# Six half-size loads, one per weight tile, in place of three whole ones before the last projection

## The chip, the cores and the metric

The kernel runs on one core of one Trainium2 chip. Its time is the device time of one execution in microseconds (us), given as the median of several runs. The engines that matter here are TensorE (PE, matmuls), ScalarE (ACT), VectorE (DVE), GpSimd (POOL) and SyncE (SP). SP and ACT each have a queue through which transfers (DMAs) are issued; the transfers of both are carried out by the same 16 DMA engines.

## The reference

One decoder layer over 256 tokens of width 2048 in float32: three gated branches, merged and projected back, and then a gated embedding, on which this case turns.

```python
def mixer_layer(x, p_i, ...):
    h = rmsnorm(x, norm_g)
    proj = h @ w_in
    ...                                    # attention A, attention B, recurrence C
    y_d = jnp.einsum('bsnc,ncd->bsnd', y, w_br)
    merged = jnp.einsum('bsnd,bsnd->bsd', gates, y_d)
    x = x + merged @ w_out
    x = x + jax.nn.sigmoid(rmsnorm(x, ple_norm_g) @ w_pg) * (p_i @ w_pp)
    return x

def reference(x, p, ...):
    ...
    return rmsnorm(x, final_norm_g)
```

`p_i @ w_pp` depends on no earlier step, and `final_norm_g` is needed only at the very end.

## The kernel before, in words

Every float32 matrix product is made as three matmuls (L185 to L187) of values split into a high part and a residual. The weights stream from DRAM in tiles of 128 x 1024 (512 KB). Each tile goes the same way: `fetch` issues its DMA on SP's queue into one of five raw buffers (`r_...`), `split` casts the high part on ACT (L136, `wh_...`) and takes the residual on DVE (L138, `wl_...`) into one of four pairs of buffers, and PE makes 12 matmuls from it. A tile's raw buffer is free again when its residual is done, its high and residual buffers when PE is done with it.

The stretch that matters is the end of the output projection `w_out` and the start of the gate's projection `w_pg`. The second half of `w_out` (named `out2` in the source, `out` in the trace) has plain tiles in two column chunks; they are called here 0_4 to 0_14 and 1_4 to 1_14, after chunk and first row block. `w_pg` follows in four column chunks of eight tiles. In the first pass the tiles 0 to 5 of its chunk 0 run, then 0 to 5 of chunk 1, and after them 6 and 7 of both. The names of both chunks read `pg_0`, `pg_1` and so on once the buffer numbers are left out, so in each list below the second `pg_0` is that of the second chunk.

When a column chunk n of the output projection is finished (n = 0 to 3), `residual` adds it into `xr` on DVE (L1081) and sums squares on ACT (L1084, `jy`). `turn_later` then turns it into the layout that `w_pg` needs: two transposes on DVE (L808, `flip_x`), four DMAs into DRAM (L812, `d_x`), one DMA back (L813, `turn_x`), and some tiles later four scalings on ACT (L1011), a cast (L1012, `x_hi`) and a residual on DVE (L1013, `x_lo`). The DMA back waits on SP's queue until the four others have landed, and whatever stands behind it on that queue waits too.

The projection of p was made at the start and parked in DRAM (`pp_d`). Two blocks of 128 x 2048 (`pps`, 1 MB each) are loaded back, and one block `fg` with the final norm's weights repeated in every partition (1 MB). The last stage, `output` and `gated`, reads both.

The order around the change is set in two ways. Within the program text an operation can be put off: `later(ticks, work)` keeps it until `tick()` has been called that often, and `tick()` is called once per weight tile, after its split. All of it is then placed on the engines' queues by a scheduler, which follows its own estimate of the times; each engine runs its list strictly in that order. DMAs draw on eight shared completion semaphores in turn, and a DMA may have to wait until the one before it on the same semaphore has landed.

Of the kernel before, what the change touches and what calls it, by code (L numbers as in the profile page):

```python
# [16 lines left out]
P = 128  # L17
D = 2048
SEQ = 256
NH = SEQ // P  # L20
BW = D // 2
# [31 lines left out]
def trunk(ctx: ExitStack, tc: tile.TileContext, x, early, table, onehot, maskv, w_in, sinks, conv, w_ri, vec, fin, w_br,  # L53
          w_out, w_pg, out):
    nc = tc.nc
# [9 lines left out]
    def block(name, dtype=F32):  # L65
        return blk.tile([P, SLOT], dtype, tag="blk", name=name)
# [74 lines left out]
    def later(ticks, work):  # L141
        timers.append([ticks, work])
# [349 lines left out]
    pp_d = dram.tile([2, P, NH, BW], F32, name="pp_d")  # L492
# [458 lines left out]
    def wide(t):  # L951
        return t[:, : NH * BW].rearrange("p (h c) -> p h c", h=NH)
# [142 lines left out]
    rms_finish(rs2, tot)  # L1095

    pps = [wide(block(f"pp{h}")) for h in range(2)]
    for h in range(2):
        nc.scalar.dma_start(pps[h], pp_d[h])

    fg = block("fg")
    nc.scalar.dma_start(fg[:, :D], bass.AP(tensor=fin.tensor, offset=fin.offset, ap=[[0, P], [1, D]]))
    HW = CW // 2
    sq3 = const.tile([P, NH, 4], F32, name="sq3")
    part = const.tile([P, NH], F32, name="part")
# [180 lines left out]
```

## Time and profile before

| | us |
|---|---|
| median of three runs | 995.31 (993.62 to 995.84) |
| profiled execution, its own time | 993.94 |
| its span in the profile | 992.1 |
| PE busy | 978.4 (99%) |
| DVE busy | 700.0 (71%) |
| ACT busy | 583.2 (59%) |
| DMA moved | 232.63 MB, 234 GB/s over the span |

Busy times are shares of the span. A busy PE is not PE at full pace: the granted clock, one digit for each fortieth of the span, stands beside it. Times inside the span are counted from its start.

### The profile page before, as it was taken

What the parts mean: (1) busy time and instruction counts of PE and PEld (TensorE: products, weight loads), DVE (VectorE), ACT (ScalarE), POOL (GpSimd) and SP (SyncE); (2) the same over time, 40 slices, a digit from 0 to 9 for tenths busy, and PEclk for the clock granted to TensorE, in tenths of its full rate; (3) what the DMA queues carried; (4) which work ended last, traced back from release to release, by engine and by line L of the source; (5) the groups of instructions that cost most, each with busy time, mean ns of one, the idle gap of its engine ahead of it and who ended that gap; (6) DMA issues with size and microseconds to landing.
All of it is one profiled execution on the core that took longest, in us unless ns stands there. A gap on an engine that the chain in (4) does not pass through costs nothing.

```text
span 992.1 us, 12462 instructions
## 1 busy us (share of the span) xinstructions
PE 978.4 (99%) x4432; PEld 814.2 (82%) x4432; DVE 700.0 (71%) x983; ACT 583.2 (59%) x818; POOL 3.4 (0%) x12
## 2 busy tenths in 40 slices
PE   9999999999999999999999999999999999989996
PEld 7888888888888888888888888888888888868886
DVE  6746875566877576576567888697589598946583
ACT  7644545557676566545466766765556465746562
POOL 0000000000000000000000000000000000000000
PEclk9999999999999999999999999999999999989999
DMA  9967877777788667637888786677748966798552
GB/s 343 323 189 227 289 225 231 220 225 233 237 251 258 222 191 242 212 128 234 252 256 273 237 250 221 214 225 234 251 153 272 343 210 214 233 347 261 186 181 85
DMA packets 83494, 232.63 MB, mean 234 GB/s; under 512 B 9400, under 2 KB 30952, under 8 KB 82920
## 3 DMA queue, kind: packets, MB, share of 16 engines
q1 hardware_dynamic: 76896, 219.32, 68.1%
q10 hardware_dynamic: 6536, 12.52, 3.6%
q8 instruction: 35, 0.57, 0.2%
q14 instruction: 27, 0.22, 0.1%
HBM read 211.06 MB, written 20.75 MB: 234 GB/s over the span
## 4 chain that ended last, share of the span: by engine, by line
PE 94%; DMA 2%; DVE 2%; ACT 1%; issue 0%; SPq 0%; DVEq 0%; ACTq 0%
PE ps_in L186 21%; PE ps_in L187 21%; PE ps_in L185 21%; PE ps_pg L185 3%; PE ps_pg L186 3%; PE ps_pg L187 3%; PE ps_out L186 2%; PE ps_out L187 1%; PE ps_out L185 1%; PE ps_bra L186 1%; PE ps_bra L187 1%; PE ps_brc L185 1%; PE ps_brc L187 1%; PE ps_bra L185 1%; PE ps_brc L186 1%; PE ps_brb L185 1%
## 5 line engine op out<-in xcount | busy, mean ns | idle before, releaser
L138 DVE TENSOR_TENSOR wl_in<-r_in,wh_in 128x1024 fp32r<-128x1024 f32 x224 | 273.2, 1221 | 152.3 <-ACT wh_in L136 146.9
L136 ACT CAST wh_in<-r_in 128x1024 fp32r<-128x1024 f32 x224 | 235.1, 1052 | 204.9 <-PE ps_in L187 170.5
L186 PE MATMUL ps_in<-wl_in,h 128*128 128x512 f32 x896 | 349.1, 390 | 0.4 <-DVE wl_in L138 0.4
L185 PE MATMUL ps_in<-wh_in,h 128*128 128x512 f32 x896 | 349.3, 390 | 0.0
L187 PE MATMUL ps_in<-wh_in,h 128*128 128x512 f32 x896 | 349.0, 389 | 0.0
L186 PEld LDWEIGHTS ps_in<-wl_in,h 128*128 128x128 f32 x896 | 168.2, 188 | 34.8 <-DVE wl_in L138 0.8
L187 PEld LDWEIGHTS ps_in<-wh_in,h 128*128 128x128 f32 x896 | 168.2, 188 | 34.8
L185 PEld LDWEIGHTS ps_in<-wh_in,h 128*128 128x128 f32 x896 | 168.3, 188 | 34.1
L138 DVE TENSOR_TENSOR wl_pg<-r_pg,wh_pg 128x1024 fp32r<-128x1024 f32 x28 | 34.3, 1223 | 24.2 <-ACT wh_pg L136 22.4
L136 ACT CAST wh_pg<-r_pg 128x1024 fp32r<-128x1024 f32 x28 | 29.5, 1053 | 29.1 <-PE ps_pg L187 20.4
L185 PE MATMUL ps_pg<-wh_pg,x_hi 128*128 128x512 f32 (+1 forms) x120 | 45.0, 375 | 0.0
L186 PE MATMUL ps_pg<-wl_pg,x_hi 128*128 128x512 f32 (+1 forms) x120 | 45.0, 375 | 0.0
L187 PE MATMUL ps_pg<-wh_pg,x_lo 128*128 128x512 f32 (+1 forms) x120 | 45.0, 375 | 0.0
L185 PE MATMUL ps_out<-wh_out,m_hi 128*128 128x512 f32 x96 | 38.7, 403 | 2.7 <-ACT wh_out L136 2.7
L136 ACT CAST wh_out<-r_out 128x1024 fp32r<-128x1024 f32 x24 | 25.1, 1052 | 27.3 <-PE ps_out L187 12.8
L138 DVE TENSOR_TENSOR wl_out<-r_out,wh_out 128x1024 fp32r<-128x1024 f32 x24 | 29.2, 1218 | 14.4 <-ACT wh_out L136 14.4
L186 PE MATMUL ps_out<-wl_out,m_hi 128*128 128x512 f32 x96 | 38.7, 403 | 0.5 <-DVE wl_out L138 0.5
L187 PE MATMUL ps_out<-wh_out,m_lo 128*128 128x512 f32 x96 | 38.3, 399 | 0.0
L138 DVE TENSOR_TENSOR wl_brc<-r_brc,wh_brc 128x1024 fp32r<-128x1024 f32 x16 | 19.6, 1222 | 20.2 <-ACT wh_brc L136 20.2
L136 ACT CAST wh_brc<-r_brc 128x1024 fp32r<-128x1024 f32 x16 | 16.9, 1055 | 25.1 <-PE ps_in L187 25.1
L136 ACT CAST wh_brb<-r_brb 128x1024 fp32r<-128x1024 f32 x16 | 16.9, 1054 | 23.4 <-PE ps_brb L187 9.4
L138 DVE TENSOR_TENSOR wl_brb<-r_brb,wh_brb 128x1024 fp32r<-128x1024 f32 x16 | 19.3, 1218 | 11.1 <-ACT wh_brb L136 11.1
(362 smaller groups left out, 1356.3 us busy)
## 6 DMA issues: line engine op xcount, KB each, us to landing
r_in<-w_in_dram SPq DMA_DIRECT2D x228, 512.0 KB, 4.5
r_pg<-w_pg_dram SPq DMA_DIRECT2D x32, 512.0 KB, 4.5
r_out<-w_out_dram SPq DMA_DIRECT2D x28, 512.0 KB, 4.8
r_brc<-w_br_dram SPq DMA_DIRECT2D x16, 512.0 KB, 3.6
r_bra<-w_br_dram SPq DMA_DIRECT2D x16, 512.0 KB, 4.3
r_brb<-w_br_dram SPq DMA_DIRECT2D x16, 512.0 KB, 4.4
d_b<-flip_b SPq DMA_DIRECT2D x32, 96.0 KB, 2.9
turn_b<-d_b SPq DMA_DIRECT2D x8, 384.0 KB, 4.9
```

Source lines behind the costliest of these rows:

```text
L136: casts.append(nc.scalar.copy(hi[:, c], r[:, c]).ins)
L138: los.append(nc.vector.tensor_tensor(lo[:, c], r[:, c], hi[:, c].bitcast(F32), op=ALU.subtract).ins)
L185: nc.tensor.matmul(ps, ah, bh, start=first, stop=False, **more)
L186: nc.tensor.matmul(ps, ah, bl, start=False, stop=False, **more)
L187: nc.tensor.matmul(ps, al, bh, start=False, stop=last, **more)
```

## The change

The two loads of the parked projection and the one of the final norm's weights are cut into six of 128 x 1024 (512 KB). They are no longer issued where they stand in the program but put off with `later`: the first comes at the second tick from there on, which is that of the second tile of `w_pg`, and one more at each tile after it.

```diff
     pps = [wide(block(f"pp{h}")) for h in range(2)]
-    for h in range(2):
-        nc.scalar.dma_start(pps[h], pp_d[h])
-
     fg = block("fg")
-    nc.scalar.dma_start(fg[:, :D], bass.AP(tensor=fin.tensor, offset=fin.offset, ap=[[0, P], [1, D]]))
+    rows = [(pps[h][:, i, :], pp_d[h][:, i, :]) for h in range(2) for i in range(NH)]
+    rows += [(fg[:, i * BW : (i + 1) * BW], bass.AP(tensor=fin.tensor, offset=fin.offset + i * BW, ap=[[0, P], [1, BW]]))
+             for i in range(2)]
+    for n, (to, src) in enumerate(rows):
+        later(2 + n, lambda to=to, src=src: nc.scalar.dma_start(to, src))
```

The amount of data and the reading side stay as they are. On ACT's queue, around the end of the first column chunk of the output projection, there stands before (casts of weight tiles, and the three DMAs):

```order
L1012 CAST x_hi<-turn_x_7100 128x1024
L136 CAST wh_out_0_14_7310<-r_out_0_14_7308 128x1024
L1099 DMA pp_7473<-pp_d 128x2048
L1099 DMA pp_7474<-pp_d 128x2048
L1102 DMA fg<-fin_dram 128x2048
L136 CAST wh_out_1_4_7342<-r_out_1_4_7340 128x1024
L136 CAST wh_out_1_6_7360<-r_out_1_6_7358 128x1024
```

After the change the three DMAs are gone from there, and the casts of tiles 0_14 and 1_4 follow each other. On the same queue, at the first tiles of `w_pg` before:

```order
L136 CAST wh_pg_1_7505<-r_pg_1_7503 128x1024
L136 CAST wh_pg_2_7529<-r_pg_2_7527 128x1024
L136 CAST wh_pg_3_7547<-r_pg_3_7545 128x1024
L1084 ACTIVATE jy_7455,sq_6831<-xr_6822 128x512 x2
L136 CAST wh_pg_4_7565<-r_pg_4_7563 128x1024
L1011 ACTIVATE turn_x_7330<-turn_x_7330,vecs 128x2x4x32 x4
L136 CAST wh_pg_5_7583<-r_pg_5_7581 128x1024
L1012 CAST x_hi<-turn_x_7330 128x1024
L136 CAST wh_pg_0_7601<-r_pg_0_7599 128x1024
```

`turn_x_7330` is the turned chunk n = 2. The same place after the change:

```order
L136 CAST wh_pg_1_7502<-r_pg_1_7500 128x1024
L1011 ACTIVATE turn_x_7330<-turn_x_7330,vecs 128x2x4x32 x4
L136 CAST wh_pg_2_7527<-r_pg_2_7525 128x1024
L1012 CAST x_hi<-turn_x_7330 128x1024
L1103 DMA pp_7473<-pp_d 128x1024 x2
L136 CAST wh_pg_3_7546<-r_pg_3_7544 128x1024
L1103 DMA pp_7474<-pp_d 128x1024
L1084 ACTIVATE jy_7455,sq_6831<-xr_6822 128x512 x2
L136 CAST wh_pg_4_7565<-r_pg_4_7563 128x1024
```

The scalings of chunk n = 2 moved from behind the cast of tile 4 to ahead of that of tile 2, and the first three of the six DMAs stand around the cast of tile 3. The last two, on the same queue, with the semaphores that each row waits for (`DMAHW` and a number are those of DMAs):

```order
L1103 DMA fg<-fin_dram 128x1024 [waits DMAHW1_49]
L136 CAST wh_pg_0_7603<-r_pg_0_7601 128x1024 [waits DMAHW0_49,PE_49,Activation_49]
L1103 DMA fg<-fin_dram 128x1024 [waits DMAHW6_49]
L136 CAST wh_pg_1_7622<-r_pg_1_7620 128x1024 [waits DMAHW2_49,DVE_49,PE_49]
L136 CAST wh_pg_2_7646<-r_pg_2_7644 128x1024 [waits DVE_49,PE_49]
```

The second half of `fg` waits for semaphore 6, which the DMA of `r_pg_2` of the second chunk raises; so ACT reaches the cast of `pg_1` of that chunk only when that later tile has landed. On SP's queue, at the fetches of these tiles, before:

```order
L812 DMA d_x_7334<-flip_x_7331 32x4x256 x4
L110 DMA r_pg_3_7545<-w_pg_dram 128x1024
L110 DMA r_pg_4_7563<-w_pg_dram 128x1024
L110 DMA r_pg_5_7581<-w_pg_dram 128x1024
L110 DMA r_pg_0_7599<-w_pg_dram 128x1024
L813 DMA turn_x_7330<-d_x_7334 128x1024
L110 DMA r_pg_1_7617<-w_pg_dram 128x1024
```

And after the change:

```order
L812 DMA d_x_7462<-flip_x_7459 32x4x256 [waits DMAHW0_49]
L812 DMA d_x_7462<-flip_x_7459 32x4x256 [waits DMAHW2_49]
L812 DMA d_x_7462<-flip_x_7459 32x4x256 [waits DMAHW3_49]
L110 DMA r_pg_3_7662<-w_pg_dram 128x1024 [waits DMAHW4_49,DVE_49]
L110 DMA r_pg_4_7680<-w_pg_dram 128x1024 [waits DMAHW5_49,DVE_49]
```

These are the last three transfers of chunk n = 3 and the two fetches behind them. Semaphore 2 is raised by `r_pg_1` of the second chunk, 3, 4 and 5 by the second, third and fourth of the new loads, so SP waits there for ACT's transfers to land. Further up on the same queue `turn_x_7330` now stands right behind the fetch of tile 3, with tiles 4, 5 and 0 behind it:

```order
L110 DMA r_pg_3_7544<-w_pg_dram 128x1024
L813 DMA turn_x_7330<-d_x_7334 128x1024
L110 DMA r_pg_4_7563<-w_pg_dram 128x1024
L110 DMA r_pg_5_7582<-w_pg_dram 128x1024
L110 DMA r_pg_0_7601<-w_pg_dram 128x1024
```

It moved ahead of those three fetches.

## The prediction

> **What bounds the kernel now.** I read the page first, for the engine that carries the end and for the slice where it does not.
>
> ```profile
> PEclk9999999999999999999999999999999999989999
> DMA  9967877777788667637888786677748966798552
> PE 94%; DMA 2%; DVE 2%; ACT 1%; issue 0%; SPq 0%; DVEq 0%; ACTq 0%
> ```
>
> TensorE (PE) is 94% of the chain that ended last, so a change pays only where PE stands still or runs slowly. The granted clock leaves 9 in one slice alone, the 36th of 40 (24.8 us each: 868 to 893 us), which is also a slice in which the DMA engines are at 9. The waits between 850 and 993 us name what PE lacks there.
>
> ```profile
> ACT wh_out L136 <- DMA r_out<-w_out_dram: 10.6, 2, 10.1
> PEld ps_out L185 <- ACT wh_out L136: 3.2, 1, 3.2
> PE ps_out L185 <- ACT wh_out L136: 2.7, 1, 2.7
> ```
>
> ScalarE (ACT) waited 10.1 us at one stroke for a weight tile of w_out, and PE waited 2.7 us for that cast. PE's own timeline gives the whole price; these are the last matmul before the gap, the first two behind it, the first back at full pace, and a later one.
>
> ```profile
> 875.69 0.39 PE L187 MATMUL ps_out<-wh_out,m_lo 128*128 128x512 f32 x1
> 878.82 0.76 PE L185 MATMUL ps_out<-wh_out,m_hi 128*128 128x512 f32 x1 [2.74 <-ACT wh_out L136]
> 880.08 0.80 PE L186 MATMUL ps_out<-wl_out,m_hi 128*128 128x512 f32 x1 [0.50 <-DVE wl_out L138]
> ...
> 886.24 0.39 PE L186 MATMUL ps_out<-wl_out,m_hi 128*128 128x512 f32 x1
> ...
> 891.91 0.39 PE L187 MATMUL ps_out<-wh_out,m_lo 128*128 128x512 f32 x1
> ```
>
> At full pace a matmul starts every 0.227 us (25 of them from 886.24 to 891.91: 5.67/25). The next was due at 875.92 and came at 878.82: 2.90 lost. The second came 1.26 later instead of 0.23: 1.03 lost. From 880.08 to 886.24 there are 15 intervals, worth 3.40 at full pace, which took 6.16 at mostly half clock: 2.76 lost. Together 2.90 + 1.03 + 2.76 = 6.69 us. From 886.24 on PE is dense until the tail, so the whole end of the kernel stands 6.69 us later for it.
>
> The chain says why the tile was late: SyncE's queue (SP) waits for the landing of d_x (the flipped chunk on its way through DRAM) before it may issue turn_x (the way back); the fetch of r_out tile 1_6 stands behind that and then takes 11.53 us.
>
> ```profile
> 859.16 6.36 DMA d_x<-flip_x
> ...
> 865.66 0.34 SPq L813
> ...
> 866.09 11.53 DMA r_out<-w_out_dram
> ...
> 877.73 1.05 ACT wh_out L136
> ```
>
> What it shared the engines with stands in ACT's timeline and in the windows (busy times, then the granted clock, the DMA share and GB/s).
>
> ```profile
> 864.19 0.33 ACTq L1099 DMA_DIRECT2D pp<-pp_d  x1
> 864.86 0.33 ACTq L1099 DMA_DIRECT2D pp<-pp_d  x1
> 865.23 0.44 ACTq L1102 DMA_DIRECT2D fg<-fin_dram  x1
> ```
>
> ```profile
> 865.00:870.00 5.00, 5.00 (x23) 4.14 (x23) 3.33 (x3) 1.52 (x2) 0.00 (x0) 1.00 0.93 362
> 870.00:875.00 5.00, 5.00 (x23) 4.13 (x22) 0.00 (x0) 0.00 (x0) 0.00 (x0) 1.00 1.00 415
> 875.00:880.00 5.00, 1.84 (x6) 0.82 (x4) 1.20 (x1) 1.76 (x2) 0.00 (x0) 0.89 1.02 414
> 900.00:905.00 5.00, 5.00 (x24) 4.14 (x23) 3.04 (x5) 4.25 (x8) 0.69 (x1) 1.00 0.90 266
> 920.00:940.00 20.00, 20.00 (x90) 16.56 (x89) 11.03 (x12) 9.90 (x14) 0.00 (x0) 1.00 0.62 192
> ```
>
> The three transfers that the change touches were issued 1.2 us before SP's, and for the next 15 us the engines ran full: 5 x (362 + 415 + 414) = 5.96 MB.
>
> **The change part by part.** First, what leaves the crowded stretch.
>
> ```profile
> r_pg<-w_pg_dram SPq DMA_DIRECT2D x32, 512.0 KB, 4.5
> pp<-pp_d ACTq DMA_DIRECT2D x2, 1024.0 KB, 4.9
> fg<-fin_dram ACTq DMA_DIRECT2D x1, 1024.0 KB, 12.1
> ```
>
> Two loads of pp and one of fg are 3 x 1.05 = 3.15 MB of those 5.96. What stays is 2.8 MB, 7 us at 400 GB/s, so that SP's own requests would be through near 873 instead of 880. Ahead of tile 1_6 there is then only turn_x: two transfers of 0.52 MB, 2.9 us at the 362 GB/s of the first window. When must it land? Its cast takes 1.05 and the residual on VectorE (DVE) 1.23 behind it, so for PE at 875.92 it must have landed by about 873.5. The same tile's fetches between 845 and 930 us took (shortest, median, longest):
>
> ```profile
> DMA to landing us min/median/max: 4.6/8.2/13.8
> ```
>
> With 4.6 it lands at 870.7, with the median 8.2, most of it measured in the crowd, at 874.3, 0.8 too late. I take a value near the lower end, since the crowd is what leaves: no stall. The gain's ends are 6.69 and 6.69 - 0.8 = 5.9.
>
> Second, six transfers instead of three. An issue takes ACT's queue 0.33 to 0.44, with 0.67 from one to the next; at the new place ACT runs in the rhythm of one tile in 2.72 us:
>
> ```profile
> 890.97 1.05 ACT L136 CAST wh_pg<-r_pg 128x1024 fp32r<-128x1024 f32 x1 [1.66 <-PE ps_out L187]
> 893.69 1.05 ACT L136 CAST wh_pg<-r_pg 128x1024 fp32r<-128x1024 f32 x1 [1.67 <-PE ps_out L187]
> 892.06 1.22 DVE L138 TENSOR_TENSOR wl_pg<-r_pg,wh_pg 128x1024 fp32r<-128x1024 f32 x1 [1.50 <-ACT wh_pg L136]
> 896.38 0.23 PE ps_pg L185
> ```
>
> 1.66 us of each turn is idle, and two issues are 1.34: nothing. Without that cover three more issues would cost 3 x 0.67 = 2.0 us of ACT.
>
> Third, 3.15 MB beside the w_pg fetches. A raw tile's buffer is free when the residual ends (892.06 + 1.22 = 893.28, 2.3 behind its cast), the fetch five tiles on starts then, and that tile's cast comes 5 x 2.72 = 13.6 after the first cast: 11.3 us for a landing of 4.5. The cast itself is ahead of PE by 8.1 us (pg_1 is cast at 890.97, and PE, which starts the tile before it at 896.38, comes to it at 899.10), of which cast and residual need 2.3. So a landing may be late by 6.8 us before ACT notices and by 12.6 before PE does. How late can it be? In the 12.5 us from 865 to the landing at 877.6 about 5 x 362 + 5 x 415 + 2.6 x 414 = 4.96 MB moved, 3.15 of them ACT's; SP got 1.8, or 145 GB/s where a tile in 2.72 us needs 192 (as from 920 to 940). ACT's 3.15 MB at the other 252 GB/s take 12.5 us, and a fetch at 145 instead of some 300 loses at most about 6 us. Ends: 0 and 6, under the 12.6; on PE's path nothing. Here the rows from 900 to 905 (0.90 busy at 266 GB/s) leave less free than 920 to 940 does, which is why this stays a rival.
>
> The Trainium skill, "DMA: Bandwidth & Descriptors", section "Rules for kernel authors", speaks against the split: it wants 1 MiB and more per DMA. By the same page's fit of about 2.0 us plus bytes over 436 GB/s, three more transfers would be an estimated 6 us more of transfer time, and the sum, if all of it were uncovered, 0.7 us of gain, a change too small to measure, which is counted with C below. The rows agree only for a transfer alone; in the crowd above transfers of 512 KB and 1 MB together filled the engines at 415 GB/s.
>
> Fourth, what moves with it. The turned chunk n = 2 (its SP issue, four scalings on ACT) now stands ahead of the cast of pg_2 instead of behind that of pg_4, and ACT waits there for its landing. Before:
>
> ```profile
> 883.77 1.30 DVE L808 STREAM_TRANSPOSE flip_x<-xr 128x512 f32<-128x512 f32 x2
> 885.10 1.94 SPq L812 DMA_DIRECT2D d_x<-flip_x  x4
> 893.81 0.33 SPq L813 DMA_DIRECT2D turn_x<-d_x  x1
> 900.62 1.71 ACT L1011 ACTIVATE turn_x<-turn_x,vecs 128x256 f32<-128x256 f32 x4 [0.39 <-DMA turn_x<-d_x]
> ```
>
> Landings of d_x and then of turn_x in the same stretch:
>
> ```profile
> DMA to landing us min/median/max: 3.4/4.2/8.8
> DMA to landing us min/median/max: 5.7/6.8/8.8
> ```
>
> Without the stall PE starts tile 1_6 at 875.92 and each next one 2.72 later: pg_2 at 894.96. The cast of 1_10 waits for a buffer that PE frees at 873.2; 1.05 for it, then the residual with the addition into xr beside it until about 876.0, and 1.30 for the flips: 877.3. d_x is issued in 1.94, until 879.2, and lands by 883.4, turn_x lands by 890.2; scalings 1.71, cast 1.05 and residual 1.23 end at 894.2. That is 0.8 us in time by the medians, 2.7 by the shortest, and with both longest (6.6 more) 5.8 us late: the thinnest cover of all. I take the medians, so no cost; a stop here could bring the half pace with it.
>
> Fifth, the waits that ride on shared DMA semaphores. The second half of fg waits for the landing of r_pg_2 of the second column chunk, with the cast of pg_1 of that chunk queued behind it and DVE and PE behind the cast. That fetch starts when the residual of the first chunk's pg_3 is done, three DVE operations of some 1.2 us behind 894.2, at 897.8, and lands 4.5 to 10.5 later (third step), 902.3 to 908.3; PE needs the cast to start by 908.56 - 2.3 = 906.2. That is 3.9 in time to 2.1 late; the r_pg row is the nearer one, so no cost. SP's third d_x of chunk n = 3 waits for a w_pg tile likewise, with pg_3 of that chunk behind it (PE at 914.0).
>
> Last, pp is first read in the gated stage, and lands some 20 us before:
>
> ```profile
> 935.45 1.26 ACT L1112 ACTIVATE y<-ps_pg,rs 128x512 f32<-128x512 f32 x2
> ```
>
> Sum, against the profiled execution's 993.94 us (span 992.1 and 1.8 around it): 993.94 - 6.69 = 987.25. The median of the runs is 995.31, 1.4 above it, within 993.62 to 995.84; if that spread is the stall's own it goes too, if it lies elsewhere 988.6 is left. I forecast 987.6, nearer to the first.
>
> **The rivals.** A: a short stop comes back, at pg_2 through the moved chunk, or because tile 1_6 lands at 874.3. For it: the covers of 0.8 us. Against it: the traffic around 880 to 890 is then lighter than the one in which the medians were measured. Price: 1 us of idle gives 988.3; with the half clock behind it (1.03 + 2.76) 992. The Trainium skill, "TensorE: Matmul & The Clock Gate", section "What's actually happening", puts the fall of the clock behind an idle window of about 3.4 us. By that rule 1 us would cost only itself; this trace shows the fall after only 2.9 us, so the rule's limit is not met exactly, but its sense agrees.
>
> B, the other side: the six transfers crowd the w_pg fetches into a larger stop than the one removed. Place: pg_3 of the second chunk, whose fetch stands on SP behind d_x and, through it, behind a landing. Its landing is due by 914.0 - 2.3 = 911.7; only 4.9 us later than that (2.9 idle as before and the 2.0 that count as slower) does it decide. With SP at 145 GB/s the fetch that it waits for, issued at 894.2, lands 10.5 later at 904.7, and pg_3 by the median of 8.2 at 912.9: 1.2 us of idle. For a slower kernel it needs 5 and the half clock: 987.25 + 4.9 + 1.03 + 2.76 = 996 us. The span from 892 to 908 would have to carry 3.15 MB, five tiles (2.6) and d_x and turn_x (1.05) in 16 us, 425 GB/s, just over the 415 seen.
>
> C: no change. The fetch of 1_6 was late because SP stood 6.36 us behind d_x, which the change leaves. For it: those 6.36 us are more than half of what PE has in hand. Against it: 7.4 us are left from the fetch at 866.09 to 873.5, and 4.6 do. It needs a landing of 11.5 us again with no crowd beside it: 994.
>
> **How the numbers follow.** Forecast 0.68, A 0.17, B 0.08, C 0.07. A change under 0.2% (2 us) can't be told from none here, so faster means below 993.3: the forecast, and A except 0.02 of it. Faster 0.83, same 0.09, slower 0.08. The range 986.3 to 991.5 takes the forecast with its 5.9 and its 988.6 and most of A, and leaves out B, C and A's worst.
>
> **What would show it.** Right: no granted clock below 9 in the 36th slice, ACT's wait on r_out gone from 10.1 to under 2, 1_6 landing in under 8 us, PE dense from 860 to 975, the span near 985.4. The fourth step is wrong if PE waits on the cast of pg_2; the third and fifth if it waits on pg_1 to pg_3 of the second chunk; the first if the fetch of 1_6 still takes over 8 us. A slow start or tail that moves alone would make the sum wrong with every step right.

## The result, and the profile after

The changed kernel takes 988.18 us (987.6 to 988.87, four runs) against 994.72 (993.62 to 995.84, four runs) of the kernel before in the same comparison: the ratio is 0.9935, with a 95% interval of 0.9917 to 0.9954, so 6.5 us less (4.6 to 8.3). The forecast was 987.6 in a range of 986.3 to 991.5.

The page of the kernel after, its row of granted clock and its row of DMA, each in 40 slices:

```profile
PEclk9999999999999999999999999999999999999999
DMA  9967877677777767746788777667748966689642
```

The slice in which the clock fell to 8 is gone. The waits between 850 and 990 us show that ACT still waits for w_out's tiles, but PE, which had a row of 2.7 us here, has none for an operand:

```profile
ACT wh_out L136 <- DMA r_out<-w_out_dram: 4.2, 3, 3.7
ACT wh_pg L136 <- DMA d_x<-flip_x: 3.9, 1, 3.9
ACT turn_x L1011 <- DMA turn_x<-d_x: 3.2, 2, 2.0
ACT wh_pg L136 <- DMA r_pg<-w_pg_dram: 2.6, 3, 1.4
```

The windows at the old place and at the new one (PE's busy time first, then PEld, DVE, ACT and POOL, the granted clock, the DMA share and GB/s):

```profile
865.00:870.00 5.00, 5.00 (x24) 4.15 (x23) 4.33 (x4) 3.00 (x4) 0.00 (x0) 1.00 0.53 162
870.00:875.00 5.00, 5.00 (x24) 4.15 (x23) 1.46 (x2) 1.93 (x2) 0.00 (x0) 1.00 1.02 416
875.00:880.00 5.00, 5.00 (x24) 4.14 (x23) 4.87 (x6) 4.79 (x11) 0.00 (x0) 1.00 0.89 283
...
900.00:905.00 5.00, 5.00 (x24) 4.15 (x23) 1.23 (x1) 1.06 (x2) 0.36 (x1) 1.00 1.01 387
905.00:910.00 5.00, 5.00 (x23) 4.14 (x23) 3.59 (x3) 2.44 (x3) 0.00 (x0) 1.00 1.02 407
910.00:915.00 5.00, 5.00 (x23) 4.13 (x23) 1.23 (x1) 3.64 (x7) 0.00 (x0) 1.00 1.03 408
```

PE is busy all through. Of the full stretch from 865 to 880 us only 870 to 875 is left, and the engines are now full from 890 to 915 us, where no tile is late enough for PE to wait. In ACT's timeline the cast of tile 1_6, then the turned chunk n = 2 ahead of pg_2, and the second half of fg with the cast behind it:

```profile
872.85 1.05 ACT L136 CAST wh_out<-r_out 128x1024 fp32r<-128x1024 f32 x1 [3.71 <-DMA r_out<-w_out_dram]
...
888.86 1.71 ACT L1011 ACTIVATE turn_x<-turn_x,vecs 128x256 f32<-128x256 f32 x4 [2.05 <-DMA turn_x<-d_x]
890.47 1.03 ACT L136 CAST wh_pg<-r_pg 128x1024 fp32r<-128x1024 f32 x1
...
903.94 0.34 ACTq L1103 DMA_DIRECT2D fg<-fin_dram  x1
904.40 2.00 ACT L136 CAST wh_pg<-r_pg 128x1024 fp32r<-128x1024 f32 x2 [3.94 <-DMA d_x<-flip_x]
```

The cast waits 3.71 us where it waited 10.1, and PE comes to the tile at 877.40 without a gap. Tile 1_6 (issued at 867.04) landed 5.7 us after its issue instead of 11.5.

The profiled execution took 988.87 (span 987.1), 5.1 below that of before, while PE's loss at tile 1_6 fell from 6.7 to nothing. Of the missing 1.6, PE lost 1.4 at 783 to 791 us (its intervals between matmuls against 0.227), in a stretch that the change does not touch, where PE waited for w_br's residuals (its timeline):

```profile
784.09 0.51 PE L186 MATMUL ps_brb<-wl_brb,zb_hi 128*128 128x512 f32 x1 [0.32 <-DVE wl_brb L138]
790.66 0.50 PE L186 MATMUL ps_brb<-wl_brb,zb_hi 128*128 128x512 f32 x1 [0.29 <-DVE wl_brb L138]
```

The profiled execution of the kernel before had no loss there. The fifth and sixth experiments below come back to this.

### The profile page after: what moved, and what is told of

The parts are those of the page before. It is cut to its first block, busy times and chain, and to the rows that moved or that the text cites. A ratio compares the mean times of both kernels' runs of the same rounds, so it can differ in the third digit from the quotient of the medians.

```text
span 987.1 us, 12467 instructions
## 1 busy us (share of the span) xinstructions
PE 975.4 (99%) x4432; PEld 812.0 (82%) x4432; DVE 699.4 (71%) x983; ACT 582.2 (59%) x818; POOL 4.3 (0%) x12
## 4 chain that ended last, share of the span: by engine, by line
PE 94%; DMA 3%; DVE 1%; ACT 1%; issue 1%; SPq 0%; DVEq 0%; ACTq 0%
PE ps_in L186 20%; PE ps_in L187 20%; PE ps_in L185 20%; PE ps_pg L187 3%; PE ps_pg L186 3%; PE ps_pg L185 3%; PE ps_out L186 2%; PE ps_out L187 2%; PE ps_out L185 2%; PE ps_bra L186 1%; PE ps_brc L187 1%; PE ps_bra L185 1%; PE ps_bra L187 1%; PE ps_brc L185 1%; PE ps_brc L186 1%; PE ps_brb L186 1%
## 5 line engine op out<-in xcount | busy, mean ns | idle before, releaser
L136 ACT CAST wh_out<-r_out 128x1024 fp32r<-128x1024 f32 x24 | 25.2, 1051 | 21.3 <-PE ps_out L187 10.1
```

The lines of the kernel that those rows point to most:

```text
L136: casts.append(nc.scalar.copy(hi[:, c], r[:, c]).ins)
```

## The experiments

**1. The place alone: whole transfers, put off.** The three transfers stay whole and are put off by `later`. Apart from ACT's queue the order differs from the changed kernel's only behind 905 us, where the turned chunk n = 3 stands one tile later on SP and DVE.

```diff
-    for n, (to, src) in enumerate(rows):
-        later(2 + n, lambda to=to, src=src: nc.scalar.dma_start(to, src))
+    for h in range(2):
+        later(2 + h, lambda h=h: nc.scalar.dma_start(pps[h], pp_d[h]))
+    later(4, lambda: nc.scalar.dma_start(fg[:, :D], ...))
```

> The three whole transfers (1 MB each) are put off to the second, third and fourth tile of w_pg instead of being cut into six; on every engine but ScalarE's queue the order is that of the changed kernel. Theory (the place decides: 3.15 MB beside the fetch of w_out's tile 1_6 made it late): no stop of TensorE at that tile, 988.2 us as with six, within 1 us; wait of ScalarE on r_out under 4 us, granted clock 1.0 throughout. Rival (the halving decides, since 512 KB pieces let SyncE's fetches through sooner): the whole transfers crowd the w_pg fetches as they did the w_out ones, a stop of some us returns at w_pg's second chunk, 990 to 995 us.

Measured: 987.26 us, ratio 0.9937 (0.9925 to 0.9949). Its longest wait of ACT for w_out was a little over the forecast's 4:

```profile
ACT wh_out L136 <- DMA r_out<-w_out_dram: 5.5, 3, 4.7
```

No stop of PE from 860 us on, though the three were issued within 1.4 us, at 890.76 to 892.13. The place brings the whole gain; the halving is not needed for it.

**2. The halving alone.** The six are issued at once where the three stood.

```diff
-        later(2 + n, lambda to=to, src=src: nc.scalar.dma_start(to, src))
+        nc.scalar.dma_start(to, src)
```

> The six half-size transfers are issued at once where the three whole ones stood; all other queues have the order of the kernel before. Theory (the place decides): the same 3.15 MB in the same stretch, so the stop at tile 1_6 stays, TensorE idle 2 to 3 us and half clock behind it, 994.7 us within 1. Rival (the halving decides): tile 1_6 lands by 873.5 us, no stop, 988 us. In between (row size sets the shares of the two queues): landing 1 to 2 us sooner than with whole ones, 990 to 993 us.

Measured: 994.34 us, ratio 1.0012 (1.0 to 1.0023). The stop stayed, but the trace shows that it has a second cause here. PE's stop, and ACT's timeline at the last two of the six:

```profile
878.66 0.50 PE L185 MATMUL ps_out<-wh_out,m_hi 128*128 128x512 f32 x1 [3.49 <-ACT wh_out L136]
879.92 0.80 PE L186 MATMUL ps_out<-wl_out,m_hi 128*128 128x512 f32 x1 [0.76 <-DVE wl_out L138]
...
872.93 4.24 ACTq L1103 DMA_DIRECT2D fg<-fin_dram  x2
877.56 2.94 ACT L136 CAST wh_out<-r_out 128x1024 fp32r<-128x1024 f32 x3 [10.82 <-DMA fg<-fin_dram]
```

The two halves of fg stand ahead of the cast of tile 1_6, and each waits for a shared semaphore: ACT's queue stood until 877.2, though tile 1_6 had landed 10.1 us after its issue at 864.93, at 875.0. So this run mixes the crowd with a wait that the three whole transfers did not have, and that the time came out as expected is partly luck. By these figures the crowd alone would have stopped PE too: it was due at the tile at 875.0, just when the tile landed, and cast and residual take 2.3 us. Experiment 7 takes that wait out.

**3. No loads at all.** The last stage reads xr in place of pp and fg.

```diff
-    for h in range(2):
-        nc.scalar.dma_start(pps[h], pp_d[h])
     fg = block("fg")
-    nc.scalar.dma_start(fg[:, :D], ...)
+    pps = xr
+    fg = xr[0].rearrange("p h c -> p (h c)")
```

> The loads of the parked projection and of the final norm's weights are left out altogether; the last stage reads xr in their place, so part of the computation is changed. Theory (the six transfers cost nothing at their new place): 988 us, not more than 0.5 below the changed kernel. Rival (they still cost there, through the wait of ScalarE before a cast and the full DMA engines): 985 to 987 us.

Measured: 988.2 us, ratio 0.9948 (0.9936 to 0.996), the time of the changed kernel. It is no clean floor, for it has a stop of its own: the scheduler set the scalings of the turned chunk n = 3 ahead of the cast of pg_2 of the second chunk, where the changed kernel has them behind pg_4.

```profile
909.16 1.71 ACT L1011 ACTIVATE turn_x<-turn_x,vecs 128x256 f32<-128x256 f32 x4 [7.74 <-DMA turn_x<-d_x]
...
911.85 0.51 PE L185 MATMUL ps_pg<-wh_pg,x_hi 128*128 128x512 f32 x1 [0.65 <-ACT wh_pg L136]
913.11 0.50 PE L186 MATMUL ps_pg<-wl_pg,x_hi 128*128 128x512 f32 x1 [0.75 <-DVE wl_pg L138]
```

ACT waits 7.74 us for the landing, the casts behind it are late, and PE loses 1.95 us: what rival A feared for chunk n = 2, at chunk n = 3 and with no load beside it. The granted clock did not fall. Without this loss and one of 0.24 us near 789 us its span of 987.2 would be 985.0, which is also the span of experiment 5, with all six loads and no loss. So the loads cost nothing at the new place that these runs can show.

**4. Doses at the old place.** Of the three whole transfers, fg alone, or pp's two alone, stays at the old place; the rest is put off in halves.

```diff
     fg = block("fg")
+    nc.scalar.dma_start(fg[:, :D], ...)         # one kernel: fg early, pp's halves later(2) to later(5)
+    for h in range(2):                          # the other: pp early, fg's halves later(2), later(3)
+        nc.scalar.dma_start(pps[h], pp_d[h])
```

> A dose: only fg's 1 MB is issued at the old place, the four halves of pp stay put off. Theory (bytes beside tile 1_6's fetch make it late, some 400 GB/s): 1.05 MB take 2.6 us of full engines instead of 7.6, so the tile lands 5 us sooner than in the kernel before, near 872.7 us where 873.5 is needed: no stop or under 0.5 us, no half clock, 987 to 988.5 us. Rival (it is the issue of any transfer there, or fg's read of one row 128 times, not the bytes): a stop of 2 us and more, 991 to 994 us.

> A dose: pp's two transfers of 1 MB are issued at the old place, fg is put off in two halves. Theory (bytes): 2.1 MB take 5.1 us of full engines, tile 1_6 lands some 2.5 us sooner than in the kernel before, near 875.1 us, 1.6 too late: TensorE idles 1 to 2 us; if the granted clock stays at 1.0 then 988.5 to 990 us, if it falls for one window 991 to 993 us. Rival (fg is the one that crowds): no stop, 987 to 988 us. Rival (order of the turned chunks, not the transfers, set the gain): 994 us.

Measured: 987.18 us with fg early, ratio 0.9924 (0.9905 to 0.9942), and 990.55 with pp early, 0.9964 (0.995 to 0.9979). ACT's longest wait at tile 1_6, first with 1 MB and then with 2 MB at the old place:

```profile
872.16 1.05 ACT L136 CAST wh_out<-r_out 128x1024 fp32r<-128x1024 f32 x1 [4.99 <-DMA r_out<-w_out_dram]
```

```profile
874.96 1.05 ACT L136 CAST wh_out<-r_out 128x1024 fp32r<-128x1024 f32 x1 [7.49 <-DMA r_out<-w_out_dram]
...
876.06 0.50 PE L185 MATMUL ps_out<-wh_out,m_hi 128*128 128x512 f32 x1 [0.17 <-ACT wh_out L136]
877.32 0.50 PE L186 MATMUL ps_out<-wl_out,m_hi 128*128 128x512 f32 x1 [0.76 <-DVE wl_out L138]
```

The first load, fg, adds little: in the seven other profiles that have no load at the old place this wait is 3.1 to 4.8 us. Two more add 5.1 us to the wait (4.99, 7.49 and, with all three, 10.1) and 5.0 to the time from the tile's issue to its landing (6.5, 9.7 and 11.5). That is 2.5 us each on average, what 1.05 MB take at some 415 GB/s. Up to 5 us cost nothing, 7.5 cost PE 1.48 us at full clock, and 10.1 cost 6.7 with the half clock. Pp early was run a second time:

> The kernel with pp early in two wholes once more, on the same chip as the one with halves: 989 to 991 us, a loss of TensorE of 1 to 2 us at tile 1_6, and in some executions a fall of the granted clock behind it.

Measured: 989.96 (0.9958, 0.9945 to 0.997); PE lost 1.52 us. No fall of the clock was in either profile. The mean granted clock, noted with every run, is 0.997 or 0.998 in all ten runs of the changed kernel; 3.4 us at half clock would lower it by 0.0017 (an estimate, half of 3.4 in 987). It is 0.996 in one of the first seven runs (991.71 us) and in one of the six later ones (991.47): there the clock probably fell.

**5. One burst at the new place.** All six put off to the same tick.

```diff
-        later(2 + n, lambda to=to, src=src: nc.scalar.dma_start(to, src))
+        later(2, lambda to=to, src=src: nc.scalar.dma_start(to, src))
```

> All six half-size transfers are put off to one tick, that of w_pg's second tile, so they come as one burst in the new place. Theory (a w_pg landing may be up to 12 us late there before TensorE stops): no stop, 987 to 988.5 us as with one per tile, ScalarE waits some us before casts. Rival (one per tile is what hides them): the burst of 7.6 us of full engines makes a tile of the second chunk late, TensorE stops 1 us and more, 989 to 994 us.

Measured: 988.25 us, ratio 0.9934 (0.9915 to 0.9954), no stop of PE. ACT waited for w_pg's tiles instead, 8.3 us in five waits, the longest 3.1:

```profile
ACT wh_pg L136 <- DMA r_pg<-w_pg_dram: 8.3, 5, 3.1
```

Spacing them one per tile is not needed either: the room ahead of PE covers the burst, which was issued from 891.1 to 895.9 us where the changed kernel's six take from 890.6 to 904.3. Here, and in the profiles of experiments 1 and 4 with fg early, PE lost nothing at 783 to 791 us. Pp early lost nothing there in its first profile and 1.1 us in its second, so that loss comes and goes with the execution.

**6. The same remedy at the next crowd.** The four loads of xr on ACT's queue at 768 to 773 us, put off one per tile, on top of the change.

```diff
-            nc.scalar.dma_start(xr[i][:, h, :], x[h * P : (h + 1) * P, i * BW : (i + 1) * BW])
+            later(1 + NH * i + h, lambda i=i, h=h: nc.scalar.dma_start(
+                xr[i][:, h, :], x[h * P : (h + 1) * P, i * BW : (i + 1) * BW]))
```

> The changed kernel, with the four loads of the residual stream (xr, 512 KB each, on ScalarE's queue at 768 to 773 us) put off in the same way, one per tile of the following stage, since the changed kernel's profile has TensorE lose 1.6 us at 784 to 791 us beside them. Theory (the same cause: they crowd the fetches of w_br): that loss goes where an execution has it, 986.8 to 988 us, 0.5 to 1 below the changed kernel's 988.2. Rival (the loss is the b_out loads' and the raw buffers', not theirs): no difference to the changed kernel; and if the new place crowds w_out instead, 989 us or more.

> The kernel with xr's loads put off too, once more, beside the changed kernel on one chip. If xr's loads cost the changed kernel time in some executions, it is 0.5 to 1.2 us below the changed kernel's time of this call; if that difference was the chip's or chance, within 0.4 us of it.

> The changed kernel once more, for the comparison with the one that spreads xr's loads: 987 to 988.5 us; its profile has a loss of TensorE near 784 to 791 us in some executions and not in others (theory: chance of the DMA's timing), and none from 860 us on.

Measured: 986.94 us at first (0.9933, 0.9921 to 0.9945); then, side by side, 987.49 (0.9929, 0.9914 to 0.9944) against 988.1 of the changed kernel (0.9936, 0.992 to 0.9952). ACT's wait for w_br between 770 and 800 us, in the changed kernel's second profile and, with xr's loads put off, in the one taken beside it:

```profile
ACT wh_brb L136 <- DMA r_brb<-w_br_dram: 8.3, 3, 6.3
```

```profile
ACT wh_brb L136 <- DMA r_brb<-w_br_dram: 3.7, 2, 2.2
```

The wait shrinks and in both its profiles PE loses nothing there, while the changed kernel lost 1.4 (the expectation says 1.6) and 1.9 us in its two. That says little: of the eleven profiles with xr's loads at the old place only three lost more than 1 us. Also, the order of other instructions changed, and the difference in time, 0.6 us, is within the intervals: that this version is the fastest is not shown.

**7. Halves against wholes, without the semaphore's wait.** As experiment 4 with pp early, but pp in four halves; on SP, DVE and PE the order is the same.

```diff
-        nc.scalar.dma_start(pps[h], pp_d[h])
+        for i in range(NH):
+            nc.scalar.dma_start(pps[h][:, i, :], pp_d[h][:, i, :])
```

> As the kernel with pp early (2.1 MB at the old place, fg put off in two halves), but pp in four halves instead of two wholes, and no fg transfer whose semaphore holds ScalarE's queue; every other queue has the same order. Theory (bytes alone): tile 1_6 lands as with two wholes, ScalarE waits 7 to 8 us for it, TensorE loses about 1.5 us, 990.5 us within 1. Rival (rows of 4 KB instead of 8 KB give SyncE's fetches a larger share): the tile lands 1 to 2 us sooner, TensorE loses under 0.5 us, 987.5 to 989 us.

Measured: 991.22 us, ratio 0.9975 (0.9964 to 0.9987), against 989.96 with wholes in the same comparison. ACT waited longer, not shorter, and PE lost 2.91 us:

```profile
875.54 2.17 ACT L136 CAST wh_out<-r_out 128x1024 fp32r<-128x1024 f32 x2 [8.94 <-DMA r_out<-w_out_dram]
...
876.64 0.50 PE L185 MATMUL ps_out<-wh_out,m_hi 128*128 128x512 f32 x1 [1.61 <-ACT wh_out L136]
```

Tile 1_6 landed 10.1 us after its issue, with wholes 9.7 and 9.2. Halves do not let SP's fetches through sooner. That they are worse is not shown: PE was due at the tile 9.5 us after the fetch's issue here, with wholes 10.5 and 10.0, so there was less room. The median also holds what this profile does not show: the mean granted clock is 0.997 in the profiled run and 0.996 or less in six of the eight, with wholes in one of six.

## Why the prediction was right

**The sum.** PE's loss of 6.69 us was to go, and it went: no gap from 860 us on, the clock at 1.0. The measured 6.5 us agree. That the bytes beside it made tile 1_6 late is shown by the doses; that the place and not the halving brings the gain, by experiments 1 and 7. The reordered queues that came with the change are not what brings it: but for the three loads the list of every engine is the same before and after as far as tile 1_10, and pp early has a reordered start of w_pg as well, and its stop is there.

**The first step** said 4.6 to 8.2 us for the landing and took a value near the lower end; it was 5.7. The test named for it, a wait of ACT under 2 us, was mis-sized: it was 3.7, and by the prediction's own rows it would have been 3.0 (ACT free at 867.66, the landing at 870.7). A wait up to 5 us costs nothing (fg early), since a cast may start long before PE needs it.

**The second and third steps** held: the extra issues cost nothing, and the w_pg landings in the crowd came to at most 7.7 us, 3.2 above the 4.5 of the sum, where 6 were allowed. Their shortest, median and longest from 845 to 930 us, after and then before:

```profile
DMA to landing us min/median/max: 3.4/5.0/7.7
```

```profile
DMA to landing us min/median/max: 3.8/4.9/6.0
```

The prediction's estimate from the Trainium skill, "DMA: Bandwidth & Descriptors", three more transfers costing 6 us if nothing covered them, has no trace here: six transfers and three took the same time at the new place (988.18 and 987.26, ratios of 0.9935 and 0.9937 in two comparisons). That page gives the fit behind it for transfers issued from GpSimd, and these go through ACT's queue. The runs can't tell what a transfer costs alone.

**The fourth step** was right in its sign and too narrow. The cover at pg_2 was put at 0.8 us; the scalings waited only 2.05 us, since turn_x, issued at 885.25, had landed by 888.86, in 3.6 us where the median of 6.8 from the crowded trace was taken. With PE at tile 1_6 at 877.40 it comes to pg_2 seven tiles later, at 896.44, and the residual ended at about 892.8: 3.6 us in hand. Experiment 3 shows that the mechanism is real.

**The fifth step** was right in the place and in the cost, with two errors that cancel. The second half of fg held ACT until 903.94 (forecast 902.3 to 908.3, on a clock 1.5 us earlier), PE needed the cast by 877.40 + 12 x 2.72 - 2.3 = 907.7, and it began at 904.40. The profile puts this wait down to d_x; by ACT's list it is for r_pg_2, which was issued at 896.19, some 3 us earlier than forecast on that clock, and took 7.7 us to land where the sum took 4.5.

**Rival C** was right that SP's wait behind d_x made the fetch late. The fetch of 1_6 waits on SP's queue for the raw buffer of tile 0_10, whose residual in the kernel before is

```profile
859.48 1.22 DVE L138 TENSOR_TENSOR wl_out<-r_out,wh_out 128x1024 fp32r<-128x1024 f32 x1
```

The buffer was free at 860.7 and the fetch went at 866.09, 5.4 us later. The change left this wait: in the changed kernel the buffer was free at 862.2 and the fetch went at 867.04. What failed is the rival's last step, a landing of 11.5 us without the crowd: it took 5.7. So the late fetch alone makes no stop; with the crowd beside it, it does. An earlier fetch would have gone ahead of the three loads, issued at 864.2 to 865.2; that this alone would have saved the 6.7 us is likely, and no run shows it.

**The base.** 987.25 was the sum for the profiled execution and 988.87 was measured; 1.41 of the 1.62 between them are the loss at 783 to 791 us, which was in no row of before. The prediction left open whether the spread of before was the stall's own. In part it was: of 52 runs of before whose mean granted clock is noted, the 24 at 0.994 took 994.7 us on average and the 18 at 0.996 took 993.4. In part it lies elsewhere: the changed kernel's ten runs, all at 0.997 or 0.998, still range from 986.4 to 989.4. The forecast's place between 987.25 and 988.6 fits that.

## What to carry to other kernels

A transfer that is not urgent still costs if it is issued where an urgent stream has the least room: count the bytes that will be in flight, divide by what the engines move when full, and compare with the time between the stream's landing and its use. Put such transfers off to a stretch with that much room; their size and spacing did not matter there. Ask also why the urgent fetch goes out late. An issue that waits for a shared semaphore holds the work behind it on its engine (10.8 us in experiment 2), so read the order of the issuing engine's list too.

## What the runs showed of the hardware

The half clock lasted for different times behind similar stops. In the kernel before, 2.9 us without a matmul, one matmul and then another 0.5 us of waiting were followed by half clock. These are the microseconds in which it fell and came back, first in the kernel before and then in experiment 2, with a longer wait of 3.49 us (the third figure from the end is the granted clock):

```profile
878.00:879.00 1.00, 0.18 (x1) 0.18 (x1) 0.20 (x1) 0.77 (x1) 0.00 (x0) 0.94 1.03 414
885.00:886.00 1.00, 1.00 (x4) 0.80 (x3) 0.94 (x2) 1.00 (x3) 0.00 (x0) 0.64 0.88 221
...
879.00:880.00 1.00, 0.24 (x2) 0.08 (x1) 1.00 (x2) 1.00 (x2) 0.00 (x0) 0.69 1.01 381
882.00:883.00 1.00, 1.00 (x4) 0.76 (x4) 1.00 (x2) 0.95 (x4) 0.00 (x0) 0.60 0.85 295
883.00:884.00 1.00, 1.00 (x6) 0.83 (x5) 1.00 (x3) 1.00 (x3) 0.00 (x0) 1.00 0.96 373
```

A mean of 0.94 is 0.12 us at half clock, one of 0.64 is 0.72. Between them lie six microseconds at 0.50, so the half clock lasted 6.8 us in the kernel before, and by the same count 3.4 us in experiment 2. So PE lost 6.7 us with the shorter wait and 6.1 with the longer. Waits of 1.61 and 0.76 us in a row left the clock alone in experiment 7's profile, though six other runs of that kernel have a lower mean clock. The Trainium skill, "TensorE: Matmul & The Clock Gate", section "What's actually happening", lets a free-running window of about 3.4 us decide; 3.4 and 6.8 us at half clock agree with one window and two.
